# Computing the second layer's weight remainders once, during the first layer, in a two-layer fp32 decoder step

## The chip, the cores and the metric

The kernel runs on one core of a Trainium2 chip. The metric is the device time of one execution in microseconds (us). Three runs of the kernel before gave 2585.53, 2589.89 and 3289.04 us, so its median is 2589.89 us.

## The reference, cut to what matters

Two decoder layers act on 1088 tokens (1024 of a prompt and 8 samples of 8) of width 1024. Each layer adds three things to the stream `h`: a token mixer, a gated feed-forward part and a gated projection of a side input `p`. Layer 0 mixes with a short convolution of 3 taps, layer 1 with a Conformer module whose convolution has 31 taps.

```python
h = h + mix
h = h + swiglu_ffn(rms_norm(h, g_ffn[i]), ffn_w_gu[i], ffn_w_down[i])
gate = jax.nn.sigmoid(rms_norm(h, g_ple[i]) @ ple_w_gate[i])
h = h + gate * (p[i] @ ple_w_proj[i])

def swiglu_ffn(x, w_gu, w_down):      # 1024 -> 2 x 2816 -> 1024
    g, u = jnp.split(x @ w_gu, 2, axis=-1)
    return (jax.nn.silu(g) * u) @ w_down
```

At the end there is one more RMS norm. All inputs and results are fp32.

## The kernel before, in words

Activations lie transposed: the 1024 channels are 8 tiles (`h0` to `h7`) of 128 partitions, tokens along the free dimension. All weights are cut into **units** of eight 128 x 128 blocks, 512 KB each. There are 208 different units, in one DRAM tensor `wall`; the list `order` names them in the order in which TensorE uses them. The first 98 entries are the mixer and the feed-forward part of layer 0. There all 1088 tokens go through together (group GJ), so that each unit is used once. Everything behind (the rest of layer 0 and layer 1, called "the second half" below) treats the first 512 tokens (group GA) and the other 576 (GB) one after the other, and most of its units are listed twice: 226 entries of `order` for 110 different units.

TensorE multiplies in a reduced format (fp32r), so each fp32 weight is split into a rounded part `whi` and a remainder `wlo` = weight - `whi`; activations are split likewise. A block then takes three products: `whi` with both activation parts, and `wlo` with the rounded one (`block`). For each unit, `prep_to` does this: SyncE's queue (SP) loads the raw unit into `wraw` (`fetch_to`, two buffers), ScalarE (ACT) copies it to `whi`, GpSimd (POOL) subtracts to make `wlo`. `whi` and `wlo` have three buffers each. At the beginning of unit U, unit U+2 is prepared; its buffers are those of unit U-1, and its raw buffer is asked for again at once, for unit U+4. In the last feed-forward part there are five buffers and four raw ones.

The program is written out engine by engine in one fixed order, and each engine and each queue works in that order. A small cost table (`Paced`, `Engines`) estimates how far each engine is; VectorE's (DVE's) convolution taps and the like wait in a list (`bg`, `lanes`), and `after` issues them when DVE's and POOL's estimates lie behind TensorE's.

In the second half POOL also does the adds for seven of the convolution's 31 taps (`prod`), sums of squares (`sqacc`) and a product in the gate (`t<-t,r`). SP's queue also holds the stores of results (`yT`, `sb_p`, `sb_s`) and of the side projection (`pp`), in program order between the loads of weights. Names in the rows: `hn` and `hna` are split normalised activations, `act` and `cact` split hidden ones, `p` the split side input, `sh`, `sl` a split sum, `acc` the convolution's sum, `ub` and `ua` the convolution's inputs, `ps` a PSUM buffer, `ones` the matrix that sums over partitions. In the profile nearly all instructions carry one line, that of the recording helper (L121), so tiles tell them apart. L172 issues the loads of weights, L582 the stores of `pp`, L659 and L660 those of `sb_p` and `sb_s`, L827 those of `yT` in `final`.

Of the kernel before, what the change touches and what calls it, by code (L numbers as in the profile page):

```python
# [13 lines left out]
F32 = mybir.dt.float32  # L14
F32R = mybir.dt.float32r
AF = mybir.ActivationFunctionType
ALU = mybir.AluOpType
PSUM = bass.MemoryType.PSUM

P = 128  # L20
D = 1024
KD = D // P
# [46 lines left out]
class Group:  # L69


    def __init__(self, off, n, chunks, base, width):
        self.off, self.n, self.chunks, self.base, self.width = off, n, chunks, base, width
# [64 lines left out]
class Net:  # L138
# [3 lines left out]
    def __init__(self, ctx, tc, xT, wall, pT, sa, sb, vecs, yT, sa_p, sa_s, sb_p, sb_s):  # L142
        self.ctx, self.tc, self.nc = ctx, tc, Engines(tc.nc)
        self.xT, self.wall, self.pT, self.sa, self.sb, self.vecs = xT, wall, pT, sa, sb, vecs
        self.yT, self.sa_p, self.sa_s, self.sb_p, self.sb_s = yT, sa_p, sa_s, sb_p, sb_s
        first = list(range(N_UNITS_0))
        middle = list(range(N_UNITS_0, N_UNITS_0 + N_PLE + N_PW1))
        proj = list(range(middle[-1] + 1, N_UNITS - N_UNITS_1))
        rest = list(range(N_UNITS - N_UNITS_1, N_UNITS))
        pw1 = middle[-N_PW1:]  # L150
        self.order = first + middle + middle[:-N_PW1] + proj[:1] + pw1 + proj[1:] + 2 * rest + rest[-KD:]
        self.raw, self.hi, self.lo = {}, {}, {}
        self.n_raw = self.n_prep = self.blk = 0
        self.bg = deque()
        self.spare = []
        self.slots = deque(["w"] * self.RING)
        self.shift_late = True
        self.sums_split = True
        self.lanes = [deque(), deque()]
        self.lane_cost = [0.0, HALF_TILE]  # L160
        self.pe_later = []
# [36 lines left out]
    def prep_to(self, n):  # L198

        nc = self.nc  # L200
        while self.n_prep < min(n, len(self.order)):
            u = self.n_prep
            self.fetch_to(u + 1)
            raw = self.raw.pop(u)
            kind = self.slots[0]
            self.slots.rotate(-1)
            if kind == "w":
                hi, lo = (
                    self.pw.tile([P, KD * P], F32R, name=n, tag=n, bufs=self.RING)
                    for n in ("whi", "wlo"))  # L210
            else:
                hi, lo = (
                    self.pX.tile([P, 2, TB], F32R, name=n, tag="C")
                    .rearrange("p a b -> p (a b)")[:, :KD * P] for n in ("whi2", "wlo2"))
            nc.scalar.wait(nc.tensor)
            nc.scalar.activation(hi, raw, AF.Copy)
            nc.gpsimd.wait(nc.scalar)
            nc.gpsimd.tensor_tensor(lo, raw, hi.bitcast(F32), ALU.subtract)
            self.hi[u], self.lo[u] = hi, lo
            self.n_prep += 1  # L220
            self.fetch_to(u + 1 + self.RAW + len(self.spare))
            self.hi.pop(u - len(self.slots), None)
            self.lo.pop(u - len(self.slots), None)


    def block(self, g, ps, blk, x, first, last):
# [13 lines left out]
    def item(self, g, rhs, mid=()):  # L240

        ps = self.psum(g)
        for k, x in enumerate(rhs):
            self.prep_to(self.blk // KD + len(self.slots))
            self.block(g, ps, self.blk, x, k == 0, k == len(rhs) - 1)
            self.blk += 1
            for at, f in mid:
                if at == k:
                    f()
        self.nc.vector.wait(self.nc.tensor)  # L250
        return ps[:, g.base:g.base + g.n]
# [593 lines left out]
    def run(self):  # L845
        nc, tc, ctx = self.nc, self.tc, self.ctx

        def pool(name, c=ctx, side="left", space=None, bufs=1):
            kw = {} if space is None else {"space": space}
            return c.enter_context(tc.tile_pool(name=name, bufs=bufs, side=side, reuse_waits="tile", **kw))  # L850
# [39 lines left out]
        for j in range(KD):  # L890
# [3 lines left out]
            if j == 5:  # L894
                self.prep_to(self.RING)
            if j >= self.LAG:
                self.norm_stat(GJ, j - self.LAG, nc.vector)
        for j in range(KD - self.LAG, KD):
            self.norm_stat(GJ, j, nc.vector)
        [y] = self.mixer_a(y)  # L900
        c_u.close()

        c_ya = ExitStack()

        def swap():
            c_y.close()
# [2 lines left out]
            self.pYA = pool("y_a", c_ya, side="right", bufs=KD)  # L909

        ya, yb = self.ffn(GJ, 0, y, swap=swap, groups=[GA, GB])
        c_t.close()
        c_x.close()
        c_ps.close()
# [3 lines left out]
        self.TW = TB  # L918
        c_m, c_ua, c_p, c_ps = (ExitStack() for _ in range(4))
        self.pm = pool("ps_m", c_m, space=PSUM)  # L920
        self.pd = pool("dram", space=bass.MemoryType.DRAM)
        self.pp = {}
        self.pub = pool("ub")
        self.pc = pool("conv")
# [21 lines left out]
        p, raw = {}, {}  # L946
# [30 lines left out]
        def apply_b():  # L977
            self.ln_apply(GB, [
                (j, self.pX, "C") if j < 4 else (j, px2, f"x{j}") for j in range(KD - 2)], cact_b, cost=self.COST_B)

# [34 lines left out]
    RMS_AT = {GJ: (0, 2), GA: (3, 6), GB: (1, 4)}  # L1015
    T_BUFS = 5
    COST_B = 1.6
    LAG = 3
    WARM = 12
    RB_GATE = 4  # L1020
# [119 lines left out]
```

## Time and profile before

| | us |
|---|---|
| median of three runs | 2589.89 |
| lowest of three runs | 2585.53 |
| the profiled execution's own time | 2583.08 |
| its span, first to last instruction | 2581.3 |
| TensorE (PE) busy | 2527.3 |
| GpSimd (POOL) busy | 1274.8 |
| VectorE (DVE) busy | 1178.7 |
| ScalarE (ACT) busy | 798.7 |

Busy times overlap each other, and a busy TensorE is not a TensorE at its peak. The share of an engine over the whole span hides the stages: layer 0's feed-forward part is from about 360 to 1148 us, the second half from there to the end.

### The profile page before, as it was taken

How to read it: one execution, taken by the hardware profiler on the slowest of the kernel's cores; microseconds unless marked ns; L12 is line 12 of the kernel's file. 1: busy time of each engine (PE TensorE's matmuls, PEld its weight loads, DVE VectorE, ACT ScalarE, POOL GpSimd, SP SyncE). 2: the span in 40 equal slices, each digit the busy share in tenths (PEclk: the TensorE clock that was granted, in tenths of full speed). 3: DMA queues.
4: the chain of work that ended last, by engine and by line, in shares of the span. 5: the costliest groups of instructions: out<-in, count | busy, mean ns of one | idle time of the engine just before them, and what ended most of it. 6: DMA issues, size and time to landing. Idle time of an engine off the chain costs nothing.

```text
span 2581.3 us, 35487 instructions
## 1 busy us (share of the span) xinstructions
PE 2527.3 (98%) x15062; PEld 2285.7 (89%) x15062; DVE 1178.7 (46%) x1546; ACT 798.7 (31%) x996; POOL 1274.8 (49%) x668
## 2 busy tenths in 40 slices
PE   9999999999999999999999999999999999999996
PEld 8999999999999999998788987888877899999996
DVE  5222233222221221226788885888965832222248
ACT  5111132111111111125544445434344432222244
POOL 3323244222222222236687676877866664444456
PEclk9999999999999999999999999999999999999998
DMA  3211111111111111112233342232323333222222
GB/s 131 59 43 47 37 50 50 42 42 49 41 50 41 43 48 41 50 42 74 92 117 106 95 117 82 98 98 90 98 74 114 123 129 113 82 82 83 84 80 86
DMA packets 79006, 195.16 MB, mean 76 GB/s; under 512 B 26752, under 2 KB 30208, under 8 KB 78848
## 3 DMA queue, kind: packets, MB, share of 16 engines
q1 hardware_dynamic: 77696, 190.67, 23.2%
q8 instruction: 118, 1.93, 0.3%
q10 hardware_dynamic: 1152, 2.23, 0.3%
q14 instruction: 40, 0.33, 0.0%
HBM read 182.78 MB, written 10.09 MB: 75 GB/s over the span
## 4 chain that ended last, share of the span: by engine, by line
PE 82%; DVE 11%; ACT 3%; issue 2%; POOL 1%; DMA 1%; SPq 0%; DVEq 0%; POOLq 0%; ACTq 0%
PE ps L121 82%; DVE acc L121 2%; DVE t L121 2%; DVE h L121 2%; DVE ub L121 1%; DVE hn L121 1%; POOL wlo L121 1%; DVE hna L121 1%; ACT whi L121 1%; ACT hn L121 0%; DVE nt L121 0%; DMA wraw<-wall 0%; DVE p L121 0%; ACT L121 0%; DVE ua L121 0%
## 5 line engine op out<-in xcount | busy, mean ns | idle before, releaser
L121 PE MATMUL ps<-hn,whi 128*128 128x288 f32 (+3 forms) x6528 | 1324.3, 325 | 5.4 <-ACT whi L121 2.1
L121 POOL TENSOR_TENSOR wlo<-wraw,whi 128x1024 fp32r<-128x1024 f32 (+1 forms) x324 | 795.8, 2458 | 695.6 <-ACT whi L121 679.2
L121 PEld LDWEIGHTS ps<-hn,whi 128*128 128x128 f32 x6528 | 1012.5, 189 | 93.6 <-DVE hn L121 3.2
L121 PE MATMUL ps<-hn,wlo 128*128 128x288 f32 (+3 forms) x3264 | 795.0, 325 | 2.2 <-POOL wlo L121 2.1
L121 PEld LDWEIGHTS ps<-hn,wlo 128*128 128x128 f32 x3264 | 524.9, 189 | 45.3 <-POOL wlo L121 3.3
L121 PE MATMUL ps<-act,whi 128*128 128x288 f32 (+1 forms) x2496 | 512.9, 329 | 4.3 <-DVE h L121 2.7
L121 ACT ACTIVATE whi<-wraw 128x1024 fp32r<-128x1024 f32 (+1 forms) x326 | 339.4, 1043 | 437.4 <-PE ps L121 329.4
L121 PEld LDWEIGHTS ps<-act,whi 128*128 128x128 f32 x2496 | 387.9, 189 | 43.4 <-DVE h L121 4.2
L121 DVE TENSOR_TENSOR h<-ps,h 128x1088 f32<-128x1088 f32 (+2 forms) x216 | 204.9, 951 | 244.8 <-PE ps L121 244.5
L121 POOL TENSOR_TENSOR t<-t,r 128x1088 f32<-128x1088 f32 (+2 forms) x74 | 136.2, 1841 | 347.0 <-ACT t L121 315.8
L121 PE MATMUL ps<-act,wlo 128*128 128x288 f32 (+1 forms) x1248 | 303.9, 329 | 1.1 <-POOL wlo L121 1.1
L121 DVE TENSOR_TENSOR t<-ps,t 128x1088 f32<-128x1088 f32 (+2 forms) x89 | 80.8, 908 | 419.7 <-PE ps L121 405.7
L121 DVE TENSOR_TENSOR t<-ps,r 128x512 f32<-128x512 f32 (+4 forms) x138 | 106.9, 777 | 313.0 <-PE ps L121 312.4
L121 PEld LDWEIGHTS ps<-act,wlo 128*128 128x128 f32 x1248 | 198.9, 189 | 19.5 <-POOL wlo L121 1.5
L121 ACT ACTIVATE t<-t 128x512 f32<-128x512 f32 (+4 forms) x106 | 75.8, 716 | 427.9 <-DVE t L121 427.8
L121 ACT ACTIVATE act<-t 128x1088 fp32r<-128x1088 f32 (+2 forms) x74 | 62.5, 844 | 443.9 <-DVE t L121 443.9
L121 POOL TENSOR_TENSOR sqacc<-sqacc,sq 128x512 f32<-128x512 f32 (+4 forms) x76 | 124.3, 1636 | 94.9 <-ACT sq L121 91.6
L121 POOL TENSOR_TENSOR prod<-prod 128x512 f32<-128x512 f32 x96 | 129.8, 1360 | 56.8 <-ACT prod L121 52.7
L121 DVE SCALAR_TENSOR_TENSOR acc<-ub,vecs_sb,acc 128x512 f32<-128x512 f32 x184 | 137.1, 746 | 4.0 <-ACT acc L121 4.0
L121 DVE SCALAR_TENSOR_TENSOR acc<-ua,vecs_sb,acc 128x512 f32<-128x512 f32 x184 | 129.0, 748 | 6.0 <-ACT acc L121 4.6
L121 PE MATMUL ps<-hna,whi 128*128 128x512 f32 x384 | 122.7, 399 | 3.4 <-ACT hna L121 2.1
L121 DVE TENSOR_TENSOR act<-t,act 128x1088 fp32r<-128x1088 f32 (+2 forms) x74 | 81.6, 1103 | 67.3 <-ACT act L121 67.3
(121 smaller groups left out, 1549.8 us busy)
## 6 DMA issues: line engine op xcount, KB each, us to landing
wraw<-wall SPq DMA_DIRECT2D x322, 512.0 KB, 3.3
h<-xT SPq DMA_DIRECT2D x8, 544.0 KB, 6.6
pp<-t SPq DMA_DIRECT2D x8, 288.0 KB, 2.5
ub<-pp SPq DMA_DIRECT2D x8, 288.0 KB, 3.7
pp<-t SPq DMA_DIRECT2D x8, 256.0 KB, 4.3
pl<-pp SPq DMA_DIRECT2D x8, 256.0 KB, 3.9
yT<-h SPq DMA_DIRECT2D x8, 256.0 KB, 2.0
yT<-h SPq DMA_DIRECT2D x8, 160.0 KB, 1.8
```

The lines of the kernel that those rows point to most:

```text
L121: return f(out, *args, **kw)
```

## The change

While layer 0's feed-forward part runs, a new function `stage` is called after each block of TensorE's work. Every 6.3 us of the cost table's time it does three steps for three different units: it loads a raw unit of the second half (`sraw`), it splits the one loaded before (`shi` on ACT, `slo` on POOL), and it stores the remainder made before that to a DRAM tile (`dlo`). All 110 units of the second half go through. Later, `prep_to` still loads the raw unit and makes `whi` on ACT, but `wlo` is loaded from the DRAM tile by SP's queue and no longer made by POOL.

```diff
+        self.to_stage = deque(dict.fromkeys(self.order[len(first):]))
...
             nc.scalar.wait(nc.tensor)
             nc.scalar.activation(hi, raw, AF.Copy)
-            nc.gpsimd.wait(nc.scalar)
-            nc.gpsimd.tensor_tensor(lo, raw, hi.bitcast(F32), ALU.subtract)
+            if self.order[u] in self.staged:
+                nc.sync.dma_start(lo.bitcast(F32), self.staged[self.order[u]])
+            else:
+                nc.gpsimd.wait(nc.scalar)
+                nc.gpsimd.tensor_tensor(lo, raw, hi.bitcast(F32), ALU.subtract)
...
+    def stage(self):
...
+        if nc.tensor.at < self.stage_at or self.pst is None:
+            return
+        self.stage_at = max(self.stage_at + self.STAGE_EVERY, nc.tensor.at - 2 * self.STAGE_EVERY)
+        done, self.staging = self.staging, None
+        if done is not None:
+            u, lo = done
+            self.staged[u] = self.pd.tile([P, KD * P], F32, name=f"dlo{u}")
+            nc.sync.dma_start(self.staged[u], lo.bitcast(F32))
+        ready = list(self.stage_raw)
+        if self.to_stage:
+            u = self.to_stage.popleft()
+            raw = self.pst.tile([P, KD * P], F32, name="sraw", tag="sraw", bufs=2)
+            nc.sync.dma_start(raw, self.wall[u])
+            self.stage_raw.append((u, raw))
+        if ready:
+            u, raw = self.stage_raw.popleft()
+            hi, lo = (
+                self.pst.tile([P, KD * P], F32R, name=n, tag=n, bufs=b) for n, b in (("shi", 1), ("slo", 3)))
+            nc.scalar.wait(nc.tensor)
+            nc.scalar.activation(hi, raw, AF.Copy)
+            nc.gpsimd.wait(nc.scalar)
+            nc.gpsimd.tensor_tensor(lo, raw, hi.bitcast(F32), ALU.subtract)
+            self.staging = u, lo
...
             self.block(g, ps, self.blk, x, k == 0, k == len(rhs) - 1)
             self.blk += 1
+            self.stage()
...
         ya, yb = self.ffn(GJ, 0, y, swap=swap, groups=[GA, GB])
+        while self.to_stage or self.stage_raw or self.staging:
+            self.stage_at = 0.0
+            self.stage()
+        self.pst = None
+        c_st.close()
...
+    STAGE_EVERY = 6.3
```

TensorE's order of instructions is the same in both kernels. In DVE's order eight instructions change places with a neighbour or a few.

POOL's order near the program's end, from the last feed-forward part's sums of squares into the first of the last gates, before (`sqacc` of 576 columns belongs to the former, of 320 to the latter):

```order
L121 TENSOR_TENSOR sqacc<-sqacc,sq 128x576
L121 TENSOR_TENSOR wlo_20166<-wraw_19924,whi_20165 128x1024
L121 TENSOR_TENSOR sqacc<-sqacc,sq 128x576 x3
L121 TENSOR_TENSOR wlo<-wraw_19984,whi 128x1024
L121 TENSOR_TENSOR sqacc<-sqacc,sq 128x576 x3
L121 TENSOR_TENSOR wlo<-wraw,whi 128x1024 x2
L121 TENSOR_TENSOR wlo_20411<-wraw_20169,whi_20410 128x1024
L121 TENSOR_TENSOR sqacc<-sqacc,sq 128x320
L121 TENSOR_TENSOR wlo_20450<-wraw_20247,whi_20449 128x1024
```

The same place with the change, and on to the end (`h_87` and `h_96` are two tiles of `h`):

```order
L121 TENSOR_TENSOR t<-t,r 128x576 x22
L121 TENSOR_TENSOR sqacc<-sqacc,sq 128x576 x7
L121 TENSOR_TENSOR sqacc<-sqacc,sq 128x320 x7
L121 TENSOR_TENSOR sqacc<-sqacc,sq 128x256 x6
L121 TENSOR_TENSOR h_87<-h_87,r 128x256
L121 TENSOR_TENSOR h_96<-h_96,r 128x256
```

No subtraction for a remainder is left between the sums; the same holds for POOL's whole second half.

SP's order in the Conformer module's first product for GB (`pw1`), where each pair of units is followed by the stores of the convolution's state, before:

```order
L659 DMA sb_p<-ub_9073 128x30
L660 DMA sb_s<-ub_9073 1024x1x30
L172 DMA wraw<-wall 128x1024 x2
L659 DMA sb_p<-ub_9166 128x30
L660 DMA sb_s<-ub_9166 1024x1x30
```

The same place with the change (line numbers have moved; L694 and L695 are the two stores, L221 is the load of a remainder, L175 that of a raw unit):

```order
L694 DMA sb_p<-ub_9957 128x30
L695 DMA sb_s<-ub_9957 1024x1x30
L221 DMA wlo<-dlo_3909 128x1024
L175 DMA wraw<-wall 128x1024
L221 DMA wlo<-dlo_3972 128x1024
L694 DMA sb_p<-ub_10050 128x30
L695 DMA sb_s<-ub_10050 1024x1x30
```

The loads of remainders stand between the stores and the raw loads, so that a store that waits holds them up too.

## Rows read from the trace of the kernel before

**Rows 1.** The page's first part: span, and TensorE's busy time.

```profile
span 2581.3 us, 35487 instructions
PE 2527.3 (98%) x15062; PEld 2285.7 (89%) x15062; DVE 1178.7 (46%) x1546; ACT 798.7 (31%) x996; POOL 1274.8 (49%) x668
```

**Rows 2.** Busy time by stage: the stretch in us, its length, busy us (and instructions) of PE, PEld, DVE, ACT, POOL, then TensorE's granted clock as a share, the DMA engines' busy share and GB/s.

```profile
360.00:1148.00 788.00, 787.30 (x4761) 718.15 (x4759) 189.58 (x146) 135.34 (x130) 237.18 (x96) 1.00 0.14 45
1148.00:1250.00 102.00, 97.44 (x466) 80.05 (x467) 65.56 (x67) 55.01 (x71) 63.04 (x28) 1.00 0.23 74
1250.00:1400.00 150.00, 149.06 (x836) 131.01 (x835) 125.47 (x168) 74.63 (x108) 116.12 (x77) 1.00 0.30 99
1400.00:1550.00 150.00, 138.32 (x949) 130.18 (x948) 126.87 (x157) 71.04 (x96) 106.17 (x63) 0.97 0.41 112
1550.00:1905.00 355.00, 354.94 (x1521) 286.24 (x1520) 277.40 (x574) 151.13 (x208) 276.25 (x160) 1.00 0.29 94
1905.00:1960.00 55.00, 50.95 (x204) 39.30 (x203) 29.81 (x34) 24.05 (x30) 33.80 (x17) 0.94 0.24 77
1960.00:2090.00 130.00, 125.26 (x741) 111.44 (x740) 91.08 (x83) 62.77 (x82) 88.49 (x43) 1.00 0.40 131
2090.00:2480.00 390.00, 390.00 (x2929) 390.00 (x2928) 91.74 (x122) 90.86 (x105) 176.61 (x83) 1.00 0.27 89
2480.00:2581.00 101.00, 77.40 (x533) 74.10 (x531) 75.00 (x95) 51.59 (x83) 62.57 (x37) 0.91 0.26 85
```

**Rows 3.** Whom TensorE waited for in the whole run: us in total, times, longest us. These are the largest nine of 18.

```profile
PE ps L121 <- ACT sh L121: 4.9, 2, 4.6
PE ps L121 <- POOL sqacc L121: 4.8, 1, 4.8
PE ps L121 <- DVE sl L121: 3.8, 4, 1.7
PE ps L121 <- POOL wlo L121: 3.6, 4, 1.8
PE ps L121 <- ACT t L121: 3.1, 1, 3.1
PE ps L121 <- DVE t L121: 3.0, 1, 3.0
PE ps L121 <- DVE h L121: 2.7, 2, 2.3
PE ps L121 <- DVE p L121: 2.6, 2, 1.8
...
PE ps L121 <- ACT hna L121: 2.1, 1, 2.1
```

**Rows 4.** Groups of instructions (count, busy us, mean ns of one, idle us of the engine before them and its releaser): POOL's remainders from 1148 us on, the same from 360 to 1148 us, and ACT's rounded copies in the whole run.

```profile
L121 POOL TENSOR_TENSOR wlo<-wraw,whi 128x1024 fp32r<-128x1024 f32 x227 | 557.9, 2460 | 230.6 <-ACT whi L121 230.4
...
L121 POOL TENSOR_TENSOR wlo<-wraw,whi 128x1024 fp32r<-128x1024 f32 x67 | 164.5, 2455 | 337.3 <-ACT whi L121 337.3
...
L121 ACT ACTIVATE whi<-wraw 128x1024 fp32r<-128x1024 f32 x322 | 337.0, 1048 | 437.4 <-PE ps L121 329.4 <-issue 81.3 <-DMA wraw<-wall 22.1
```

**Rows 5.** Timeline of the last gates, start us and length us: two of POOL's instructions, then three of DVE's.

```profile
2526.39 2.66 POOL L121 TENSOR_TENSOR wlo<-wraw,whi 128x1024 fp32r<-128x1024 f32 x1
2529.01 1.13 POOL L121 TENSOR_TENSOR sqacc<-sqacc,sq 128x320 f32<-128x320 f32 x1
...
2527.10 2.30 DVE L121 TENSOR_TENSOR t<-t,ub 128x320 f32<-128x320 f32 x1
2529.43 1.05 DVE L121 TENSOR_TENSOR h<-h,t 128x320 f32<-128x320 f32 x1
2530.41 0.48 DVE L121 TENSOR_TENSOR t<-ps,r 128x320 f32<-128x320 f32 x1
```

**Rows 6.** Two groups of DVE's instructions in the whole run, the same operation with both inputs in SBUF: in GA's feed-forward part (1605 to 1960 us), and in GB's (2090 to 2500 us).

```profile
L121 DVE TENSOR_TENSOR act<-t,act 128x512 fp32r<-128x512 f32 x22 | 26.2, 1190 | 15.4 <-ACT act L121 15.4
...
L121 DVE TENSOR_TENSOR act<-t,act 128x576 fp32r<-128x576 f32 x22 | 16.7, 758 | 16.6 <-ACT act L121 16.6
```

**Rows 7.** Loads of raw units: in the whole run with the median us to landing, and in `pw1` for GB (1440 to 1520 us), with the activations that follow them there.

```profile
wraw<-wall SPq DMA_DIRECT2D x322, 512.0 KB, 3.3
...
L121 ACT ACTIVATE whi<-wraw x13: 1041/1046/1062, 1439.8 to 1518.7; 128x1024 fp32r<-128x1024 f32 x13
...
DMA to landing us min/median/max: 3.2/3.7/7.1
```

**Rows 8.** Whom SP's queue waited for in the whole run: us in total, times, longest us.

```profile
SPq L172 <- POOL wlo L121: 2142.6, 308, 20.4
...
SPq L827 <- DVE t L121: 28.1, 6, 16.0
SPq L827 <- DVE h L121: 21.6, 9, 5.8
SPq L659 <- DVE ub L121: 12.6, 2, 12.2
SPq L582 <- DVE t L121: 9.1, 5, 3.5
SPq L582 <- ACT t L121: 6.7, 6, 2.1
```

**Rows 9.** The columns of rows 2 for 10 to 20 us, when the first inputs are loaded.

```profile
10.00:20.00 10.00, 10.00 (x56) 9.11 (x55) 8.03 (x6) 8.81 (x9) 4.08 (x2) 0.88 0.97 377
```

**Rows 10.** POOL's remainders in GA's feed-forward part (1610 to 1905 us): duration in ns (min/median/max), first and last start.

```profile
L121 POOL TENSOR_TENSOR wlo<-wraw,whi x53: 2394/2408/2862, 1613.0 to 1897.8; 128x1024 fp32r<-128x1024 f32 x53
```

More of the change, by code (lines that the diff above doesn't have):

```diff
@@ L153, in __init__ @@
         self.n_raw = self.n_prep = self.blk = 0
+        self.to_stage = deque(dict.fromkeys(self.order[len(first):]))
+        self.staged, self.staging, self.stage_raw = {}, None, deque()
+        self.pst, self.stage_at = None, 0.0
         self.bg = deque()
@@ L223, in prep_to @@
             self.lo.pop(u - len(self.slots), None)
+    def stage(self):
+        nc = self.nc
+        if nc.tensor.at < self.stage_at or self.pst is None:
[21 more added lines that the diff above has]
+            self.staging = u, lo
     def block(self, g, ps, blk, x, first, last):
@@ L901, in run @@
         c_u.close()
-        c_ya = ExitStack()
+        c_ya, c_st = ExitStack(), ExitStack()
+        self.pd = pool("dram", space=bass.MemoryType.DRAM)
+        self.pst, self.stage_at = pool("stage", c_st), nc.tensor.at
         def swap():
@@ L920, in run @@
         self.pm = pool("ps_m", c_m, space=PSUM)
-        self.pd = pool("dram", space=bass.MemoryType.DRAM)
         self.pp = {}
```

## Prediction

> **What bounds the kernel now.** I read the page's first part, then the busy times by stage, then TensorE's waits, then the timelines around the largest. The first part says that TensorE is busy for 2527.3 of 2581.3 us [rows 1]. Nothing that the change removes is TensorE's, so it can win only from TensorE's idle time. The stages show where that lies. In layer 0's feed-forward part TensorE is idle for 788 - 787.3 = 0.7 us [rows 2]. From 1148 us to the end the stretches hold 1433 us and TensorE is busy for 97.44 + 149.06 + 138.32 + 354.94 + 50.95 + 125.26 + 390 + 77.40 = 1383.4 of them, so 49.6 us are idle [rows 2]. That is the whole stake: under 2% of the run. Some of it can't be won, for the last sums and stores come after TensorE's last product, whatever POOL does.
>
> The waits say what the idle time is made of [rows 3]. Only 3.6 us are waits for a remainder by name. The others name DVE and ACT (`sl`, `t`, `h`, `p`, `hna`, `sh`) or POOL's sums (`sqacc`). The link to the remainders shows in the timeline of the last gates: POOL starts a remainder at 2526.39 and ends it at 2529.05; DVE starts `t<-t,ub` at 2527.10 and ends it at 2529.40, after 2.30 us, while a multiplication of the same size with one input in PSUM takes 0.48 [rows 5]. The next DVE instruction with two SBUF inputs stands beside POOL's sum and takes 1.05 us [rows 5]. The same pairing shows between stages: the subtraction for `act` takes 1190 ns on average at 512 columns where POOL is busy for 276.25 of 355 us, and 758 ns at 576 columns where POOL is busy for 176.61 of 390 [rows 2, 6]. So a remainder on POOL costs more than POOL's own time: it holds up DVE instructions that read two SBUF tiles, and those stand in front of TensorE's waits.
>
> **What it removes.** 226 of the 227 remainders that POOL makes from 1148 us on become loads: 226 x 2.46 = 556 us of POOL's time [rows 4]. POOL is not the bound, so what counts is the waits that hang on them.
> - Waits for `wlo` itself: 3.6 us go [rows 3].
> - The end. TensorE waits 4.6 us (the longest) for `sh` and 4.8 us for `sqacc` [rows 3]. DVE's chain for one tile of `h` there is 0.48 + 2.30 + 1.05 = 3.8 us [rows 5], about what TensorE needs for a unit, so DVE's backlog is paid at the end of both rounds. Without remainders I take each of the two SBUF instructions at the 0.48 of its neighbour: 1.4 us for a tile, and no backlog. The first wait then vanishes; of the last one the serial chain behind the last product stays, which I put at 2.5 us, five short steps of about 0.48 us. So 4.6 + 4.8 - 2.5 = 6.9 us go. Bounds: 0 and 9.4.
> - Other waits on DVE, or on ACT behind DVE: `sl` 3.8, ACT's `t` 3.1, DVE's `t` 3.0, `h` 2.7, `p` 2.6, `hna` 2.1, together 17.3 us [rows 3]. In the timelines about half stand beside a remainder; others stand beside POOL's own work for the norm before the second Conformer product, which stays. I take half, 8.7 us. Bounds: 0 and 17.3.
> - The clock. Granted shares of 0.97, 0.94 and 0.91 in the three stretches with the most idle time [rows 2] are short spells at 1.2 instead of 2.4 GHz behind TensorE's idle spells: 150 x 0.03 + 55 x 0.06 = 7.8 us of full clock in the first two; the third has most of its share after the last product. With about half of the idle spells gone I take 4 us. Bounds: 0 and 8.
>
> Together 3.6 + 6.9 + 8.7 + 4 = 23.2 us.
>
> **What it adds in layer 0's feed-forward part.** 110 x 2.46 = 270 us on POOL, which was busy for 237 of 788, and 110 x 1.048 = 115 us on ACT, which was busy for 135 [rows 2, 4]. POOL comes to 507 us (64%), ACT to 250 (32%). Both have room: POOL sat idle for 337 us before remainders, waiting for ACT, which waits for a free buffer [rows 4]. POOL's product in the gate may now stand behind one more subtraction of 2.46 us, within a unit of TensorE's time, 788 / 66 = 12 us. SP gains 110 loads and 110 stores of 512 KB: 115 MB over some 720 us, 160 GB/s, on 45 [rows 2]; while the inputs came in, the same DMA engines moved 377 GB/s [rows 9]. Its raw loads now stand behind stores that wait for POOL, but are asked for nearly two units ahead. The cover of all this is the 12 us unit. I take 1 us; bounds 0 and 10. The eight instructions that change places in DVE's order move by one to four places; I cost them at nothing.
>
> **What it adds later.** 226 loads of 512 KB. A raw load lands 3.3 us after its issue, 3.7 in `pw1` for GB, 7.1 at worst [rows 7]. The load of a remainder can start when its buffer comes free, two units before it is needed. A unit is (1897.8 - 1613.0) / 52 = 5.5 us for GA [rows 10] and (1518.7 - 1439.8) / 12 = 6.6 us in `pw1` for GB [rows 7], so the lead is 11 to 13 us against 3.3 to 7.1 of landing. Raw loads gain: they waited for POOL's remainder [rows 8] and now wait for ACT only, some 2.5 us earlier. DMA engines: a load takes 0.29 x 5.5 = 1.6 us of them in GA's feed-forward part [rows 2, 10], so the share goes from 0.29 to 0.58 there.
>
> What is new is the queue. SP works in order, and stores that wait for DVE or ACT now stand in front of remainders that are needed within two units. Those waits were 28.1 + 21.6 + 12.6 + 9.1 + 6.7 = 78.1 us [rows 8]. Before, POOL made its remainders from raw units that had already landed. In `pw1` for GB a lead of 13.2 us less 3.7 to 7.1 of landing leaves 6.1 to 9.5 us: a block longer than that is TensorE's wait. Most blocks are shorter; single ones of 12.2 and 16.0 are longer [rows 8], but DVE, which they wait for, gets faster. Bounds 0 and 78; I take 4 us, near the low end because only two listed maxima exceed the lead.
>
> **Sum.** 2583.08 - 23.2 + 1 + 4 = 2564.9 us for an execution like the profiled one. That execution lies 2.5 us under the lowest of the runs shown and 6.8 under their median, so I add 2.5: **2567 us**, 0.9% under the median of 2589.89. About 2% is what a measurement of this kernel can tell from no change.
>
> **Rivals.**
> - **The idle time re-forms.** DVE's waits move behind other work (ACT's order, POOL's remaining sums, the stores' landings) and only the 3.6 us of `wlo` and a few more go: 2583 - 6 + 5 + 2.5 = about 2585. For it: only 3.6 us name a remainder [rows 3], and DVE is busy for 125 of 150 us from 1250 on with taps that hardly change [rows 2]. Against: the 2.30 us instruction ends just behind POOL's [rows 5]. Chance 0.13.
> - **Slower: the blocked queue.** Stores that wait for DVE hold back the remainders, in `pw1` for GB, at the `pp` stores and at GA's `yT`. From a block of 6.1 to 9.5 us on, each us is TensorE's. With half of the 78.1 us (39) showing: 2564.9 + 35 + 2.5 = about 2602; with all of it 2641. For it: the maxima of 12.2 and 16.0 [rows 8]. Against: faster DVE, and two units of lead. Chance 0.13.
> - **Slower by far: two loads don't fit in a unit.** If two loads cost 3.3 us each, one after the other, a GA unit takes 6.6 instead of 5.5 us [rows 7, 10]. Some 100 units of GA lie between 1190 and 1960 us: +110, less the gain, 2565 + 110 = 2675. Against: 377 GB/s, and 1.6 us of DMA time for a load [rows 2, 9]. Chance 0.03. The Trainium skill's page "DMA: Bandwidth & Descriptors", section "Bandwidth", speaks for it: 1 MB at once is given 6.15 us, which as an estimate from that page is 0.6 us over a GA unit, or 60 us in all; by that rule the result would be near 2625, and the trace's 377 GB/s is above the 341 GB/s that the page gives for this size.
>
> **Chances.** My forecast 0.69 (its own range 2550 to 2583), re-formed idle time 0.13, blocked queue 0.13, two loads 0.03; 0.02 remain for a larger gain than the bounds of the large terms suggest, with most of the 49.6 us gone. From 2548 to 2600 lies all of the first two cases but their edges and about half of the third: a bit over 8 in 10. Faster by over 2% means under 2538, which needs nearly all idle time: 0.02. Slower by over 2% means over 2642: the two loads and the extreme of the queue, 0.04. Within 2%: 0.94.
>
> **What the profile of the changed kernel would show.** POOL's remainders from 1148 us on gone, its busy time there down by about 556 us; DVE's `t<-t,ub` of the last gates near 0.5 instead of 2.3 us, and `act<-t,act` of GA near 0.7; no wait for POOL's `wlo`, and waits for `sqacc` and `sh` at the end under 3 us together; in layer 0's feed-forward part TensorE idle for less than 3 us with POOL near 64%. Where the blocked queue is right, TensorE's waits name the load of `wlo`, and they cluster in 1400 to 1550 and 2030 to 2090 us. Where the loads don't fit, the DMA share nears 1 and such waits stand at every GA unit. I am wrong if TensorE's idle time from 1148 us on stays near 50 us, or if layer 0's part grows by more than 10.

## The result and the profile after

| | before | after |
|---|---|---|
| median of the runs, us | 2589.12 | **2618.93** |
| lowest and highest of the runs it rests on | 2585.53 to 2589.89 | 2616.91 to 2620.67 |
| the profiled execution's own time | 2583.08 | 2616.91 |

The ratio is 1.012 with a 95% interval from 1.010 to 1.0139: the change makes the kernel **1.2% slower**. The forecast was 2567 us, 0.9% faster, with a range up to 2600. It was wrong, in its sign too. The interval is much narrower than the 2% that the prediction took for the least that can be told. One of before's four runs, 3289.04, was a disturbed one and is left out of the ratio.

The page's first part, of the kernel after:

```profile
span 2615.1 us, 36216 instructions
PE 2538.8 (97%) x15062; PEld 2300.0 (88%) x15062; DVE 1091.9 (42%) x1546; ACT 911.2 (35%) x1106; POOL 992.9 (38%) x552
```

Against [rows 1], POOL has lost 282 us of work and DVE 87, as intended, and TensorE has as many instructions as before. Yet the span is 33.8 us longer. The busy times by stage say where. The columns are those of [rows 2]; the first row is layer 0's feed-forward part, which now ends near 1220 instead of 1148 us (its 4762 matmuls in the row match the 4761 of before), the second is the second half.

```profile
360.00:1220.00 860.00, 810.99 (x4762) 735.23 (x4760) 215.72 (x146) 247.22 (x240) 515.35 (x205) 0.97 0.51 175
...
1220.00:2615.00 1395.00, 1371.52 (x8167) 1240.20 (x8165) 770.51 (x1295) 581.72 (x781) 363.19 (x280) 0.99 0.54 183
```

The second half takes 1395 us where it took 1433: **38 us won**, twice the forecast. Layer 0's feed-forward part takes 860 us where it took 788: **72 us lost**, where the forecast was 1. In it TensorE is idle for 860 - 810.99 = 49.0 us instead of 0.7, and the same matmuls take 811.0 instead of 787.3 us [rows 2]. These 23.7 us are the clock: two neighbouring stretches of 50 us show a granted share of 0.90 (part of the stretch at 1.2 GHz, behind TensorE's idle spells) and then, with TensorE nearly always busy, 1.00.

```profile
500.00:550.00 50.00, 40.29 (x221) 36.29 (x222) 13.99 (x10) 12.44 (x12) 30.94 (x14) 0.90 0.57 191
550.00:600.00 50.00, 48.54 (x294) 44.02 (x292) 9.77 (x6) 14.81 (x15) 28.89 (x13) 1.00 0.54 188
```

TensorE's waits over the whole run, as in [rows 3] (us in total, times, longest), name DVE's stream tile `h` at the top, and the later loads of remainders with a single wait. The largest four:

```profile
PE ps L121 <- DVE h L121: 44.0, 7, 10.3
PE ps L121 <- DVE t L121: 5.3, 3, 2.7
PE ps L121 <- DMA wlo<-dlo: 3.2, 1, 3.2
PE ps L121 <- POOL sqacc L121: 2.7, 1, 2.7
```

DVE is busy for 215.72 of those 860 us, so it is not slow: it is late. The waits of all engines in layer 0's feed-forward part (360 to 1220 us) show whom it waits for, and whom that engine waits for:

```profile
ACT shi L121 <- DMA sraw<-wall: 487.9, 63, 12.5
...
POOL slo L121 <- ACT shi L121: 256.4, 51, 8.1
...
DVE act L121 <- ACT act L121: 129.2, 23, 11.0
DVE t L121 <- POOL t L121: 76.6, 7, 14.9
...
PE ps L121 <- DVE h L121: 44.0, 7, 10.3
```

Read from the bottom: TensorE waits for DVE, DVE for ACT's and POOL's halves of the feed-forward gate, and ACT, at the head of everything, stands for 487.9 us before `shi`, waiting for the new raw unit `sraw` to land. ACT's queue works in order. While `shi` waits, the copies behind it, which DVE and TensorE need, wait too.

Why is `sraw` so late? One turn of the timeline shows it (start us, length us, queue or engine; the brackets hold the idle time before and its releaser). Most of TensorE's instructions and most of the second of the unit's two staging steps are left out.

```profile
669.67 2.42 POOL L121 TENSOR_TENSOR wlo<-wraw,whi 128x1024 fp32r<-128x1024 f32 x1
669.75 1.29 DVE L121 TENSOR_TENSOR t<-ps,t 128x1088 f32<-128x1088 f32 x1 [11.11 <-POOL t L121]
...
672.12 0.33 SPq L175 DMA_DIRECT2D wraw<-wall  x1
672.50 0.42 SPq L242 DMA_DIRECT2D dlo<-slo  x1
...
672.97 0.43 SPq L247 DMA_DIRECT2D sraw<-wall  x1
...
679.56 1.06 ACT L121 ACTIVATE shi<-sraw 128x1024 fp32r<-128x1024 f32 x1 [11.25 <-DMA sraw<-wall]
680.52 1.09 ACT L121 ACTIVATE act<-t 128x1088 fp32r<-128x1088 f32 x1
680.69 2.35 POOL L121 TENSOR_TENSOR slo<-sraw,shi 128x1024 fp32r<-128x1024 f32 x1 [6.25 <-ACT shi L121]
...
681.65 2.55 DVE L121 TENSOR_TENSOR act<-t,act 128x1088 fp32r<-128x1088 f32 x1 [10.61 <-ACT act L121]
683.00 3.41 POOL L121 TENSOR_TENSOR wlo<-wraw,whi 128x1024 fp32r<-128x1024 f32 x1
...
684.12 2.48 DVE L121 TENSOR_TENSOR h<-ps,h 128x1088 f32<-128x1088 f32 x2
...
685.45 2.18 PE L121 MATMUL ps<-act,whi 128*128 128x288 f32 x6 [10.31 <-DVE h L121]
686.37 2.37 POOL L121 TENSOR_TENSOR slo<-sraw,shi 128x1024 fp32r<-128x1024 f32 x1
686.44 0.33 SPq L175 DMA_DIRECT2D wraw<-wall  x1
```

What SP's queue waited for before its raw loads, in the same 860 us:

```profile
SPq L175 <- POOL wlo L121: 656.6, 66, 16.4
```

Follow it around. On SP's queue the load of layer 0's own raw unit (`wraw`, L175) has to wait until POOL's `wlo` has freed the buffer; it goes out at 672.12, some 0.03 us after `wlo` ends (669.67 + 2.42 = 672.09). The load of `sraw` (L247) depends on none of that, but stands behind it, and goes out at 672.97. ACT's `shi` starts as it lands, 6.59 us later at 679.56, POOL's `slo` at 680.69, and POOL's next `wlo`, behind `slo`, runs from 683.00 to 686.41. That frees the next raw buffer: SP's next `wraw` goes out at 686.44. The turn took 0.85 (SP) + 6.59 (landing) + 1.13 (`shi`) + 2.31 (`slo`) + 3.41 (`wlo`) + 0.03 = **14.3 us, and TensorE's unit takes 12**. It is a usual turn: of the 63 between the raw loads of this part, as the timeline has their issues, 48 are longer than 12 us and the median is 14.2. After some three or four of them comes a short one of 6 to 8 us, so the mean is 13, and 66 units lose 72 us. None of the engines is full: POOL, the busiest in the loop, works for 515 of 860 us. The loop closes because three queues, each working in order, take turns at waiting for each other: SP for POOL, POOL for ACT, ACT for the transfer from SP. The finished `t` of 671.04 us lies for 9.5 us until ACT copies it at 680.52.

In the second half the change did what it says. The groups of [rows 5, 6], the second before and then both after:

```profile
L121 DVE TENSOR_TENSOR t<-t,ub 128x320 f32<-128x320 f32 x8 | 15.3, 1909 | 1.6 <-ACT t L121 1.5
```

```profile
L121 DVE TENSOR_TENSOR act<-t,act 128x512 fp32r<-128x512 f32 x22 | 16.0, 729 | 15.3 <-ACT act L121 15.3
...
L121 DVE TENSOR_TENSOR t<-t,ub 128x320 f32<-128x320 f32 x8 | 3.9, 485 | 1.5 <-ACT t L121 1.5
```

Before, the first took 1190 ns on average [rows 6] and the second 1909, with 2.30 us in the single instruction of [rows 5].

### The profile page after: what moved, and what is told of

The parts are those of the page before. It is cut to its first block, busy times and chain, and to the rows that moved or that the text cites. A ratio compares the mean times of both kernels' runs of the same rounds, so it can differ in the third digit from the quotient of the medians.

```text
span 2615.1 us, 36216 instructions
## 1 busy us (share of the span) xinstructions
PE 2538.8 (97%) x15062; PEld 2300.0 (88%) x15062; DVE 1091.9 (42%) x1546; ACT 911.2 (35%) x1106; POOL 992.9 (38%) x552
## 4 chain that ended last, share of the span: by engine, by line
PE 53%; DVE 2%; ACT 1%; DMA 1%; issue 0%; POOL 0%; DVEq 0%; SPq 0%; ACTq 0%
PE ps L121 53%; DVE t L121 0%; DMA wlo<-dlo 0%; DVE h L121 0%; DVE acc L121 0%; DMA dlo<-slo 0%; DVE act L121 0%; DVE hna L121 0%; DVE nt L121 0%; ACT ua L121 0%; ACT act L121 0%; ACT cact L121 0%; DVE nv L121 0%; POOL slo L121 0%; ACT whi L121 0%
## 5 line engine op out<-in xcount | busy, mean ns | idle before, releaser
L121 PE MATMUL ps<-act,whi 128*128 128x288 f32 (+1 forms) x2496 | 526.0, 336 | 48.3 <-DVE h L121 44.0
L121 PEld LDWEIGHTS ps<-act,whi 128*128 128x128 f32 x2496 | 398.0, 193 | 90.8 <-DVE h L121 46.4
L121 POOL TENSOR_TENSOR slo<-sraw,shi 128x1024 fp32r<-128x1024 f32 x110 | 263.7, 2398 | 306.0 <-ACT shi L121 256.4
L121 POOL TENSOR_TENSOR wlo<-wraw,whi 128x1024 fp32r<-128x1024 f32 (+1 forms) x98 | 258.7, 2641 | 159.4 <-ACT whi L121 143.3
L121 ACT ACTIVATE shi<-sraw 128x1024 fp32r<-128x1024 f32 x110 | 116.6, 1060 | 520.1 <-DMA sraw<-wall 487.9
L121 POOL TENSOR_TENSOR sqacc<-sqacc,sq 128x512 f32<-128x512 f32 (+4 forms) x76 | 117.9, 1552 | 275.1 <-ACT sq L121 274.7
L121 POOL TENSOR_TENSOR prod<-prod 128x512 f32<-128x512 f32 x96 | 124.3, 1303 | 182.8 <-ACT prod L121 182.7
L121 DVE TENSOR_TENSOR act<-t,act 128x1088 fp32r<-128x1088 f32 (+2 forms) x74 | 98.8, 1336 | 169.3 <-ACT act L121 169.3
```

The costliest lines, as they stand in the source:

```text
L121: return f(out, *args, **kw)
```

## The experiments

The kernel before, measured beside them, took 2588.82 us (median of seven runs, for the first four kernels) or 2590.43 us (one run, for the last four). Where one number is given it is one run. The four runs of kernel 4 lie within 4.9 us and the seven of the kernel before within 11, so differences of that size between single runs mean nothing.

**1. Staging without its use.** The remainders are made and stored as in the change, but never loaded; POOL makes them again. If the loss is layer 0's and the gain the second half's, this keeps the first alone.

```diff
-            if self.order[u] in self.staged:
+            if False:
```

> Staging as in the change, but the staged remainders are never loaded: POOL makes every remainder again where it is needed. Both theories: the loss in layer 0's feed-forward part stays (about 70 us over the kernel before in the stretch from 400 to 1215 us) and the gain of the second half is gone: 2589 + 68 = about 2655 us. If it is near 2590 instead, staging by itself costs nothing and the loss comes from the loads of remainders.

Measured: **2662.06 us**, 73 over before. Its first row below is layer 0's feed-forward part up to 1148 us, cut where before's ended, the second its second half:

```profile
360.00:1148.00 788.00, 735.55 (x4343) 666.72 (x4342) 200.82 (x135) 227.68 (x221) 471.52 (x187) 0.97 0.51 176
1220.00:2660.00 1440.00, 1389.03 (x8165) 1246.35 (x8165) 883.27 (x1294) 581.48 (x780) 921.64 (x506) 0.98 0.30 95
```

Within 788 us TensorE came to 4343 matmuls of 4761 [rows 2], and the second half is nearly what it was (DVE 883 us, POOL 922, 1440 us long against 1433). The staging alone is slower by as much as layer 0's part loses.

**2. The use without the staging.** Only eight units are staged, and every later load of a remainder takes one of the eight, so the loads have their full number and size; the other 102 remainders are left out.

```diff
+        self.to_stage = deque(list(dict.fromkeys(self.order[len(first):]))[:8])
...
-            if self.order[u] in self.staged:
-                nc.sync.dma_start(lo.bitcast(F32), self.staged[self.order[u]])
+            if u >= N_UNITS_0:
+                nc.sync.dma_start(lo.bitcast(F32), self.staged[N_UNITS_0 + u % 8])
```

> Only eight of the 110 units are staged, and every later load of a remainder takes one of these eight, so the right remainders are left out but the same bytes are loaded at the same places. Both theories: the loss of the first half is gone but for eight stages (under 6 us) and the gain of the second half stays: 2619 - 65 = about 2553 us. If the second half's gain was only time that the first half had pushed there, it would be near 2589.

Measured: **2546.68 us**, 42 under before. The two parts add up: 73 - 42 = 31, against 29.8 measured for the whole change. In the second half:

```profile
1148.00:2544.00 1396.00, 1373.50 (x8188) 1241.01 (x8186) 772.29 (x1296) 583.44 (x782) 363.87 (x280) 1.00 0.56 183
```

The 226 loads run at a DMA share of 0.56, and TensorE waits for one of them once, for 2.6 us. So neither the prediction's blocked queue nor loads that don't fit explain the loss.

**3. A control for the next.** To hold more raw units, the remainder is written over its raw unit, and the separate `slo` goes. The load still runs one step ahead of the split.

```diff
+            raw = self.pst.tile([P, KD * P], F32R, name="sraw", tag="sraw", bufs=5)
...
+            u, lo = self.stage_raw.popleft()
+            raw = lo.bitcast(F32)
```

> Control for the next run: the remainder is written over the raw unit (five buffers instead of two and three), still one stage between load and use. Theory A (ACT's in-order queue waits in shi for the landing of sraw, which SP issues only behind a raw load that waits for POOL): the wait stays, 2610 to 2622 us. Theory B (110 more subtractions on POOL are too much for POOL and DVE): the same. If it is under 2570, buffers were the cause.

Measured: 2613.85 us, 5 under after, which is within the spread; ACT still stands before `shi` as long as in after:

```profile
ACT shi L121 <- DMA sraw<-wall: 487.2, 63, 12.1
```

More buffers alone change nothing, so the loop does not run through a free buffer for `sraw`.

**4. Asking one step earlier.** As 3, but a unit is split two steps after its load was issued.

```diff
-        if len(ready) >= (1 if self.to_stage else 1):
+        if len(ready) >= (2 if self.to_stage else 1):
```

> As the control, but a raw unit is loaded two stages before its split instead of one. Theory A: ACT's waits for sraw fall from 490 us to under 100, TensorE's waits for DVE's h in layer 0's feed-forward part from 44 us to under 8, and the time to 2548 to 2562 us. Theory B (POOL's work, the same as before): waits for h stay over 30 us and the time over 2605 us.

Measured four times: **2550.49 us** (2547.9 to 2552.78), ratio to before 0.9845 (0.9819 to 0.9872). This is the change as meant, 1.6% faster than before and 2.6% faster than after, and nothing is left out. Its layer 0 part, then, from the view of the tile `sraw`, what the engines that use it waited for (us, times), then from the page's list of DMA issues the loads of `sraw` (count, KB, median us to landing):

```profile
360.00:1148.00 788.00, 785.80 (x4749) 716.51 (x4748) 190.82 (x144) 246.52 (x239) 499.05 (x205) 1.00 0.56 190
```

```profile
  POOL sraw L121: 212.7, 47
...
  DMA sraw<-wall: 16.1, 16
```

```profile
sraw<-wall SPq DMA_DIRECT2D x110, 512.0 KB, 6.8
```

The same 110 loads and splits are in these 788 us, and all stores but the last; ACT and POOL are nearly as busy as the prediction worked out (250 and 507), and TensorE loses 1.5 us. So theory B, that POOL's added work is too much in itself, falls. ACT now waits 16.1 instead of 488 us for `sraw`. The 212.7 us are ACT's other wait before `shi`, until POOL has finished with the single buffer of `shi`; they cost TensorE nothing that shows. The median landing of 6.8 us is that of after (6.7): the transfer is no faster, only its 6.6 us in the turn above no longer lie in the loop, and 14.3 - 6.6 = 7.7 us fit into 12.

**5 and 6. Which way does the loop close?** Two readings remained. A1: `sraw` is late because it stands behind `wraw` on SP's queue. A2: it is late because its landing of over 6 us is too long in itself. Both kernels keep the load one step ahead of the split, as 3. In 5 a third raw buffer makes SP's raw load wait for the remainder of the unit before instead of the newest one (the staging has four buffers there instead of five, and the third raw buffer is given up at unit 92):

```diff
+        self.ppl, self.spare, self.late = self.pst, ["sx"], 1
...
-            self.fetch_to(u + 1 + self.RAW + len(self.spare))
+            self.fetch_to(u + 1 + self.RAW + len(self.spare) - self.late)
```

> As the control e3 (one stage ahead), but in layer 0's feed-forward part the raw units have a third buffer, so that SP's raw load waits for POOL's remainder of the unit before and not for the newest one. Theory A1 (the staging load is late because it stands in SP's queue behind a raw load that waits for POOL's newest wlo): ACT's waits for sraw fall from 487 us to under 200 and the time to 2548 to 2575 us. Theory A2 (the landing alone, 6 us against a stage of 6.3 us of the cost table, is too long for one stage ahead): waits stay over 350 us and the time over 2595 us.

Measured: **2550.87 us**; layer 0's part is back at its length, and ACT's wait at an eighth:

```profile
360.00:1148.00 788.00, 785.87 (x4735) 716.01 (x4734) 190.52 (x144) 246.12 (x239) 501.36 (x205) 1.00 0.54 190
```

```profile
ACT shi L121 <- DMA sraw<-wall: 59.4, 18, 11.0
```

In 6 nothing changes but the queue that issues the load of `sraw`:

```diff
-            nc.sync.dma_start(raw.bitcast(F32), self.wall[u])
+            nc.scalar.dma_start(raw.bitcast(F32), self.wall[u])
```

> As the control e3 (one stage ahead), but the staging load is issued by ACT's queue instead of SP's, just before ACT's split of the unit loaded one stage earlier. Theory A1: the load no longer stands behind SP's raw load, so the time falls to 2548 to 2575 us. Theory A2: ACT runs on to the next split at once where nothing else stands between, and meets the landing of some 6 us; two such waits in a unit of 12 us: time over 2595 us.

Measured: **2547.5 us**, the lowest of the single runs that stage all units, with one wait for `sraw`:

```profile
  DMA sraw<-wall: 0.6, 1
```

One word, 66 us less than in 3. The same load in the page's list of DMA issues:

```profile
sraw<-wall ACTq DMA_DIRECT2D x110, 512.0 KB, 3.9
```

The landing is not the same in these two kernels, then: 5.1 us in 5 and 3.9 in 6, against 6.6 in 3. Both times are what A1 forecast (6 lies half a us under its range), but each edit changed both, when the load is issued and how long it takes to land, so the runs alone do not take A1 and A2 wholly apart. Nor does kernel 4, whose landing is as long as after's: its extra step would cure either. The trace of after says more. In 39 of ACT's 63 waits for `sraw`, ACT already stood there when the load was issued, and 128 of the 488 us lie before the issue. In the turn above ACT is free at 679.56 - 11.25 = 668.31, and the load goes out 4.7 us later, at 672.97. So A1 is shown: the load comes too late because of what it stands behind. The rest of the wait is landing, which ACT sees in full where the load comes that late. That a landing of 6.6 us would have done little harm if issued on time, against a step of about 6 us (two in a unit of 12), is worked out and was not tried by itself.

Being blocked is not what counts, either. In 5, SP's queue stands for 651 us in this part, against 720 in after, now mostly at the stores (505.6 us, for POOL's staging subtraction). What it waits for comes earlier, and so the loads behind it are in time.

**7 and 8. Why the second half gained twice the forecast.** The theory (C and C1 in the expectations) is that of the prediction's last gates: POOL's reading of SBUF holds up DVE's instructions with two SBUF inputs, everywhere. Into 4, with its remainders loaded, 7 puts four useless POOL subtractions beside each load, on a tile of their own, so that POOL is busy again but nobody needs its result; 8 replaces them with eight memsets, which write but read nothing.

```diff
+                for c in range(0, KD * P, 256):
+                    nc.gpsimd.engine.tensor_tensor(self.idle, self.idle, self.idle, ALU.subtract)
```

```diff
+                for c in range(0, KD * P, 128):
+                    nc.gpsimd.engine.memset(self.idle, 0.0)
```

> As e4 (two stages ahead), with POOL kept busy: beside each load of a remainder POOL makes four subtractions of 256 columns that read and write a tile of their own, about 2.4 us, and nobody needs them; ACT, DVE and TensorE have the order of e4. Theory C (in the second half a remainder on POOL costs by holding up DVE instructions with two SBUF inputs and POOL's own sums, not by its result): most of the gain of the second half goes, 2570 to 2590 us, and DVE's t<-t,ub of 320 columns is over 1 us again. Theory D (the gain is that the remainder itself, and raw units, come earlier): 2546 to 2556 us.

> As e7, but POOL's extra work is eight memsets of 256 columns, which read nothing from SBUF. Theory C1 (DVE is held up by POOL's reading of SBUF): DVE's t<-t,ub stays near 0.5 us and the time within 10 us of e4, up to waits for POOL's late sums. Theory C2 (POOL's queue being full is what counts, through the sums of squares): as e7, 2570 to 2590 us.

Measured: **2568.79** and **2555.66 us**, so 18 and 5 over kernel 4; the 5 are within the spread. The second half of 7 and two of its DVE groups, then those of 8:

```profile
1148.00:2567.00 1419.00, 1378.63 (x8174) 1244.11 (x8172) 824.41 (x1295) 583.59 (x782) 964.28 (x1184) 0.99 0.55 181
```

```profile
L121 DVE TENSOR_TENSOR act<-t,act 128x576 fp32r<-128x576 f32 x22 | 22.8, 1037 | 16.6 <-ACT act L121 16.6
...
L121 DVE TENSOR_TENSOR t<-t,ub 128x320 f32<-128x320 f32 x8 | 5.1, 643 | 1.6 <-ACT t L121 1.5
```

```profile
1148.00:2553.00 1405.00, 1376.89 (x8187) 1243.98 (x8185) 784.92 (x1296) 584.11 (x782) 921.50 (x2089) 0.99 0.55 183
```

```profile
L121 DVE TENSOR_TENSOR act<-t,act 128x576 fp32r<-128x576 f32 x22 | 16.7, 759 | 16.6 <-ACT act L121 16.6
...
L121 DVE TENSOR_TENSOR t<-t,ub 128x320 f32<-128x320 f32 x8 | 3.9, 485 | 1.5 <-ACT t L121 1.5
```

In kernel 4 the second half has DVE busy for 772 us and POOL for 365, and the two groups take 759 and 484 ns. POOL is at least as busy in 7 (964 us) and 8 (922) as before the change (923). With subtractions DVE's same instructions take 52 us more, with memsets 13. So it is what POOL reads, and not its being busy, that costs DVE time.

The 13 us are not the memsets' own either. `h<-h,t` at 576 columns takes 1194 ns on average in 8 and 870 in 4. The timeline of 8 shows which of them are long:

```profile
1393.13 2.90 POOL L223 MEMSET idle<- 128x256 f32 x8
1398.50 3.34 POOL L121 TENSOR_TENSOR sqacc<-sqacc,sq 128x576 f32<-128x576 f32 x2
...
1393.40 0.76 DVE L121 TENSOR_TENSOR h<-h,t 128x576 f32<-128x576 f32 x1
1398.69 1.85 DVE L121 TENSOR_TENSOR h<-h,t 128x576 f32<-128x576 f32 x1
```

Beside memsets it takes 0.76 us; it is long beside POOL's own sums (`sqacc`, `prod`), which the memsets have pushed to other moments. In 4 the second of these two starts at 1399.08 between two such sums and takes 0.76 us.

But 7 fell a little short of its forecasts, 2570 to 2590 us and over 1 us for `t<-t,ub`, and gives back only 18 of some 40 us. A subtraction of 256 columns lasts 0.61 us (median) where a remainder lasts 2.46, and `t<-t,ub` went from 484 to 643 ns, not back to the 1909 of before. DVE's busy time came back by about the same share, 52 of 111 us, which fits the theory without proving it. That single long instructions make up the rest is likely; the waits for `wlo` and raw units that are asked for earlier may have a part in it. None of these was tried by itself.

## Why the prediction was wrong

**Layer 0's feed-forward part: the step that failed.** The prediction wrote "Both have room", from POOL's 64% and ACT's 32%, and "The cover of all this is the 12 us unit. I take 1 us; bounds 0 and 10." It measured 72. The busy shares were right: kernel 4 has POOL at 499 of 788 us and ACT at 247, and there the cost is 1.5 us, where 1 was forecast. What failed was to take room for enough. The prediction named the raw loads that "now stand behind stores that wait for POOL", and stopped there; such waits are in after (63.8 us) and, without a loss, in kernel 6 (69.4). It did not follow what else stands on SP's queue behind a load that waits for POOL: the load of `sraw`, for which ACT then waits with all its other work behind it. [Rows 8] had the warning: SP waited 308 times, 2142.6 us in all, for POOL's `wlo`; in layer 0's feed-forward part it was 755.5 of 788 us. So SP's queue is nearly always blocked at a raw load, and whatever is added behind is issued when that block ends. The bound of 10 was wrong for the same reason: a loop longer than the unit eats up the lead of the buffers turn by turn, TensorE stops (49.0 us in all), and the clock adds its part (23.7 us). One more term was not in the sum: DVE, held up by POOL's new subtractions, is busy for 26 us more in this part of after (215.72 against 189.58). It is no cause by itself, for in kernel 4, with the same subtractions at other moments, DVE has 190.82.

**The rival "blocked queue"** had the right mechanism, an in-order queue whose waiting instruction holds up a load with nothing to wait for, and the wrong place. It was put on SP's stores in the second half, where it measured one wait of 3.2 us, against the 4 in the sum. Its 2602 has the sign of the result, from another place.

**Two loads don't fit in a unit.** False: DMA share 0.54 and 183 GB/s in the second half. The estimate from the Trainium skill's page "DMA: Bandwidth & Descriptors", section "Bandwidth", was near 2625 us, and the result lies close to it. That is chance, for experiment 2 has all of these loads and takes 2546.68 us.

**What it removes: right in kind, too small.** The waits of TensorE in the second half, from the same view of after, against the terms:

| term | forecast, us | measured, us | from |
|---|---|---|---|
| waits for `wlo` | 3.6 | 3.6 | none left |
| the end, `sh` and `sqacc` | 6.9 | 7.0 | 4.9 gone, 4.8 to 2.7 |
| other waits on DVE and ACT, 17.3 in all | 8.7 | 14.5 | 2.8 left |
| smaller waits, not in the sum | 0 | 4.9 | 9.0 to 4.1 |
| clock (the fall of TensorE's busy time, put down to it) | 4 | 11.9 | busy 1383.4 to 1371.5 |
| later loads | -4 | -3.2 | one wait |
| sum | 19.2 | 38.7 | stretch: 1433 - 1395 = 38 |

The end came out as worked out. The term "about half stand beside a remainder" was mis-sized: nearly all of these waits went. The likely reason is that DVE gained all along the second half: it is busy for 770.5 instead of 883 us, and kernel 7, which gives back half of that, has some of these waits again. The clock was given half of what two stretches showed, and its bound of 8 was too low. Kernel 4's second half begins at the same time as before's and is some 12 us ahead by 1905 us, so its stretches can be laid beside [rows 2], if not instruction by instruction. They have 1.00 where 0.97 and 0.94 stand there, and so has every slice of 50 us of kernel 4 from 1148 to 2498 us:

```profile
1400.00:1550.00 150.00, 140.20 (x953) 130.63 (x952) 106.19 (x155) 73.39 (x98) 51.67 (x40) 1.00 0.63 178
...
1905.00:1960.00 55.00, 54.66 (x235) 43.79 (x234) 29.53 (x42) 30.80 (x42) 12.54 (x10) 1.00 0.58 195
```

The rival "the idle time re-forms" is refuted by the same table: 23.5 us of idle time are left of 49.6, and the named waits fall from 39.6 to 12.8.

Two signs had been named by which the forecast would be known wrong: idle time near 50 us in the second half, which did not come, and layer 0's part growing by more than 10, which did.

## What to carry to other kernels

Before work is added to an engine with room, write down for each queue, DMA queues too, the order of its instructions with what each waits for, and go around every loop through several queues: the sum of issue, landing and execution around it must fit the period, whatever the busy shares say. A prefetch that depends on nothing doesn't belong behind an instruction that is usually blocked; put it on another queue (kernel 6), issue it a full landing time earlier (kernel 4), or let the blocker wait for something older (kernel 5). And when one stage pays and another wins, run each alone, as experiments 1 and 2: a result of +30 hid a loss of 73 and a gain of 42.

## What the runs showed of the hardware

That POOL's work stretches DVE's was expected, how far it reaches was not: without the remainders, DVE's 1295 instructions of the second half take 112 us less, with none of them changed. Kernels 7 and 8 tell reading from writing, 52 us against 13, and in 8 the long instructions stand beside POOL's own reading. The Trainium skill's page "SBUF — State Buffer", section "Who interferes with whom", states it as a rule: a DVE instruction with two SBUF inputs contends with a GpSimd instruction that reads SBUF, not with one that only writes it. The traces agree with it: the 22 subtractions for `act` at 576 columns take 759 ns on average in 4 and 8, and 1037 beside the subtractions of 7.

A load of `sraw` landed after 3.9 to 6.8 us (medians) while the staging ran at 175 to 191 GB/s, against the 3.3 of [rows 7] for the same 512 KB. At one and the same rate, 190 and 191 GB/s, it was 6.8 us in kernel 4, where it is issued on SP's queue right behind another load and a store, and 3.9 in kernel 6 on ACT's. The rate over the stage doesn't tell the landing, then; whether the queue or the closeness of the transfers before it made the difference was not tried apart.
